# A decoder-layer kernel on one core: the pooling products moved right behind the sums of u in two heads, and the conditioning bursts spread 6, 7, 7

## The chip, the cores and the metric

The kernel runs on one core of a Trainium2 chip. The time is device microseconds of one execution. The kernel before was timed three times: 1939.01, 1940.36 and 1944.08 us, median 1940.36 us. A further execution was recorded by the hardware profiler; every row of the profile comes from that one.

The engines of the core work side by side and each keeps its own order: PE (matrix products; PEld is its weight load), DVE (elementwise work on vectors), ACT (activations, copies and casts), POOL (some elementwise work; it also issues many of the DMAs), SP (issues the other DMAs). An engine never overtakes its own order: if one instruction waits, everything behind it on that engine waits too. Engines wait for each other through semaphores.

## The reference, cut to what matters

One decoder layer on 320 token columns (256 of a prompt, 64 of eight samples), in float32:

```
mod = silu(c) @ w_ada + b_ada                      # conditioning, six vectors of 2048 for each sequence
h   = rmsnorm(x) * (1 + sc1) + sh1
q, k, v, og, u, ga, gb = split(h @ w_in)           # four heads; 11 blocks of 256 columns for each head
y_a = rmsnorm(gated_linear_attention(q, k, v)) * silu(og)     # chunked, with a state for each sequence
d   = trailing_mean(u, window 2, 4, 8 or 16 by head) - u
y_b = (d @ w_pool) * pool_scale                    # the pooling products
x   = x + g1 * ((sigmoid(ga) * y_a + sigmoid(gb) * y_b) @ w_o)
x   = x + g2 * ffn(rmsnorm(x) * (1 + sc2) + sh2)
```

The attention states, the last pooling rows and the normalised output are returned as well.

## The kernel before, in words

Every weight is split into two parts, `whi` (cast by ACT, L162) and `wlo` (what is left, subtracted by DVE, L163), and every product is three matmuls (`mm3`, L177 to L179) of 128 columns of weights against 320 tokens. One projection (`proj`) makes 256 output columns from 16 blocks of input: 96 matmuls, which fill one accumulator `ps`. The accumulators of the projections come from a pool, `pmain`, that holds two; a projection can start when an accumulator has been emptied. Smaller products use another pool, `pmisc`, with four.

The mixer is the stretch between the head of the program and the product with `w_o`. It goes through the four heads. For each head a loop runs over 11 units (one projection each): in heads 1 and 2 the order is gb, gb, q, k, v, v, u, og, og, ga, ga; head 3 has gb last. Head 0 is projected in the head of the program, so its attention and pooling run beside the projections of head 1, those of head 1 beside the later units of head 1 and the first of head 2, and so on.

What runs beside is a list of closures, `queue`. `pump(RATE)` writes up to ten of them after each unit. The attention of a head is `gla_steps` (28 steps). Those that the text below names:

- `s_attP`, `s_kpn`, `s_inter`, `s_oback`: the samples' attention: a masked product (L831; mask on DVE and ACT, L835 to L838), the product with the loaded state (L854, L857; the state tiles `S0` are loaded by POOL's DMAs, L847, 1 MB each), its copy on ACT (L864), four transposes (L133) and copies on DVE (L870).
- `s_state`: new states. Four products into four tiles of `pmisc` (L884, each cleared first by a DVE memset, L879), then four DVE updates (L889) that empty them; the result goes out by a POOL DMA (L890).
- `s_att`, `s_nat`: the prompt's attention scores (DVE L745, PE L756 and L762) and transposes of v (L133).

The pooling of a head is `pool_steps`. It gives four steps `pst`: load the carried rows (L450), transpose them into u (`s_hist`, L460), transpose the last rows of u for output (`s_buf`: POOL copies L468 and L469, transposes L133, DVE copy L474, nine small POOL DMAs L476 and L477), and the window sums (`s_win`, DVE L486 to L500, then the split of d into `dh` on ACT, L353, and `dl` on DVE, L354). And it gives one step `psy`, the pooling products (`s_y`): it takes both accumulators of `pmain`, here named `psy`, makes four sets of six matmuls with `w_pool`, and empties each set by one DVE instruction (L516), which also multiplies by the gate gb. In head 0 `sig0` computes the gates first.

`ada_burst` (L317) is 16 matmuls that make a piece of `mod`. Its 2 MB of weights, `araw`, lie in one buffer during the mixer; two POOL DMAs (L285) refill it once the burst before has read it. `BURST_UNITS` says behind which units of heads 1 to 3 a burst stands, `LOAD_UNITS` where the loads are written.

The program order that all this writes is not yet the engines' order. A scheduler sets that: it goes by the program order, lets an instruction pass others when those cannot start in its own estimate of time, and hands out pool buffers in program order. A matmul that needs a `pmain` accumulator therefore comes behind the matmuls of the two accumulators that were handed out earlier.

Of the kernel before, what the change touches and what calls it, by code (L numbers as in the profile page):

```python
# [34 lines left out]
PSY = 12  # L35
# [42 lines left out]
def body(tc, A):  # L78
# [106 lines left out]
    def proj(w, col, k0, k1, xh, xl, between=None, raw=None):  # L185

        ps = pmain.tile([P, 2, 512], F32, tag="pm", name=nm("ps"))
        for c0 in range(k0, k1, 4):
            nk = min(4, k1 - c0)
            parts = [(i, c0 + j, whi, wlo) for j, whi, wlo in split_chunk(rows(w, col, c0, nk), nk, 256, raw)  # L190
                     for i in range(2)]
            for i, kt, whi, wlo in parts:
                mm3(ps[:, i, :T], whi[:, i * P:(i + 1) * P], wlo[:, i * P:(i + 1) * P],
                    xh[kt], xl[kt], kt == k0, kt == k1 - 1)
            if between:
                between(c0 - k0)
        return ps
# [91 lines left out]
    def anchor(src):  # L289

        return G.tensor_copy(tick, src).ins

    def ada_load(n, bufs, tag="big"):

        if n < len(BURSTS) and n not in ada_raw:
            sec, b, nb, k0, nk = BURSTS[n]
            t = ada_raw[n] = apool[0].tile([P, nk, nb * P], F32, tag=tag, bufs=bufs, name=nm("araw"))
            ada_want.extend((n, t, r) for r in range(0, nk, min(nk, 16 // nb)))

    def ada_all(after=None):  # L300
        while ada_want:
            ada_piece(after)

    def ada_burst():

        n = len(ada_done)
        sec, b, nb, k0, nk = BURSTS[n]
        ada_done.append(n)
        w = nb * P
        if k0 == 0:  # L310
            ada_ps[:] = [misc()]
        ps = ada_ps[0]
        first = True
        with tc.high_priority(), tc.issue_after(last_mm[0]):
            for r in range(nk - 4, -1, -4):
                for j in range(4):
                    PE.matmul(ps[32 * j:32 * j + 32, 0:w], lhsT=scT[:, k0 + r + j, :], rhs=ada_raw[n][:, r + j, :],  # L317
                              start=k0 == 0 and first, stop=k0 + nk == KT and r == 0, tile_position=(0, 32 * j))
                first = False
        if k0 + nk < KT:  # L320
            return
        pt = misc()
        for q in range(0, nb, 2):
            wq = min(2, nb) * P
            sb = apool[0].tile([P, wq], F32, tag="adasb", name=nm("adasb"))
            S.copy(sb, ps[:, q * P:q * P + wq])
            for i in range(wq // P):
                tr(pt[:, (q + i) * P:(q + i + 1) * P], sb[:, i * P:(i + 1) * P])
        blk = sec * KT + b
        V.tensor_reduce(mod[:, blk:blk + nb, :], pt[:, 0:w].rearrange("p (b j r) -> p b r j", b=nb, j=4)[:, :, 0:9, :],  # L330
                        axis=AX.X, op=ALU.add)
        if b == KT - nb:
            dst = mod[:, sec * KT:(sec + 1) * KT, :]
            bb = bada[:, sec * KT:(sec + 1) * KT].unsqueeze(2).broadcast_to([P, KT, 9])
            V.tensor_tensor(dst, dst, bb, op=ALU.add)
            if sec == 4:
                V.tensor_scalar(dst, dst, 1.0, None, op0=ALU.add)
                V.tensor_tensor(dst, dst, N2G.unsqueeze(2).broadcast_to([P, KT, 9]), op=ALU.mult)
# [30 lines left out]
    def new_group(h):  # L369
        g = G0()  # L370
        g.h = h
        g.q = gp.tile([P, 2, T], F32, tag="q", name=nm("q"))
        g.k = gp.tile([P, 2, T], F32, tag="k", name=nm("k"))
        g.v = gp.tile([P, 4, T], F32, tag="v", name=nm("v"))
        g.u = gp.tile([P, 2, UEW], F32, tag="u", name=nm("u"))
        g.gb = merged[h]
        return g

    def new_gates(g):
        g.og = gp.tile([P, 4, T], F32, tag="og", name=nm("og"))  # L380
        g.ga = merged[2] if g.h == 0 else None
# [4 lines left out]
    def evac(ps, g, kind, i, acc):  # L386
        with tc.high_priority():
            evac_now(ps, g, kind, i, acc)
# [29 lines left out]
    def gates(g, kind, i, src):  # L418
        if kind == "gb":
            S.activation(g.gb[:, 2 * i:2 * i + 2, :], src, AF.Sigmoid)  # L420
            return
        og = g.og[:, 2 * i:2 * i + 2, :]
        sg = gp.tile([P, 2, T], F32, tag="sg", name=nm("sg"))
        S.activation(sg, src, AF.Sigmoid)
        if kind == "og":
            V.tensor_tensor(og, src, sg, op=ALU.mult)
        else:
            G.tensor_tensor(og, og, sg, op=ALU.mult)

    def units(h):  # L430
        return [("q", 0, OQ + DK * h), ("k", 0, OK_ + DK * h), ("v", 0, OV + DV * h),
                ("v", 1, OV + DV * h + 256), ("u", 0, OU + 256 * h),
                ("og", 0, OOG + DV * h), ("og", 1, OOG + DV * h + 256),
                ("ga", 0, OGA + DV * h), ("ga", 1, OGA + DV * h + 256),
                ("gb", 0, OGB + DV * h), ("gb", 1, OGB + DV * h + 256)]
# [85 lines left out]
    with tc.tile_pool(name="head", bufs=1) as xp:  # L521
# [55 lines left out]
        g0 = new_group(0)  # L577
# [17 lines left out]
        for si, (k0, k1) in enumerate(SLICES):  # L595
# [11 lines left out]
            for ui, pair in enumerate(us):  # L607
# [9 lines left out]
                if last and ui == 0:  # L617
                    pst, psy = pool_steps(g0)
# [301 lines left out]
    def merge_step(g, E):  # L920
        def f():
            for e in range(4):
                o = E["o"][:, e]
                V.tensor_tensor(o, o, g.og[:, e], op=ALU.mult)
                V.tensor_tensor(g.gb[:, e], o, g.gb[:, e], op=ALU.add)
        return f

    queue = []

    def pump(n):  # L930
        for _ in range(min(n, len(queue))):
            queue.pop(0)()
# [3 lines left out]

    st, E = gla_steps(g0)
    def sig0():
        for kind in ("og", "ga", "gb"):
            for i in range(2):  # L940
                gates(g0, kind, i, getattr(g0, kind)[:, 2 * i:2 * i + 2, :])
    queue += pst + st[:PSY] + [sig0] + st[PSY:] + psy + [merge_step(g0, E)]
    RATE = 10
    BURST_UNITS = (None, (1, 3, 9, 10), (0, 2, 3, 4, 5, 7, 9, 10), (1, 2, 3, 4, 6, 7, 9, 10))
    LOAD_UNITS = (None, (0, 1, 7, 9, 10)) + BURST_UNITS[2:]
    for h in range(1, H):
        pump(RATE)
        g = new_group(h)
        st, E = gla_steps(g)
        order = units(h) if h == 3 else units(h)[9:] + units(h)[:9]  # L950
        for ui, (kind, i, col) in enumerate(order):
            if kind == "og" and i == 0:
                pump(len(queue))
                new_gates(g)
            ps = proj(win, col, 0, KT, hh, hl)
            evac(ps, g, kind, i, None)
            if kind == "v" and i == 1:
                pump(len(queue))
                queue += st
            if kind == "u":  # L960
                pst, psy = pool_steps(g)
                queue[:0] = pst
            if ui in BURST_UNITS[h]:
                ada_burst()
            if ui in LOAD_UNITS[h] and len(ada_done) < AMIX:
                ada_load(len(ada_done), 1)
                done = g.og if kind == "ga" else getattr(g, kind)
                ada_all(None if ui in BURST_UNITS[h] else anchor(done[:, 2 * i, PB:PB + 1]))
            pump(RATE)
            if kind == "v" and i == 0:  # L970
                pump(len(queue))
                queue += [st.pop(0) for _ in range(4)]
                pump(len(queue))
        queue += psy + [merge_step(g, E)]
    pump(len(queue))


# [196 lines left out]
```

## Time and profile before

| | |
|---|---|
| median of three runs | 1940.36 us |
| profiled execution | 1944.37 us, span from first to last instruction 1942.6 us |
| mean granted TensorE clock | 0.995 |
| PE busy | 1895.9 us (98%) |
| DVE, ACT, POOL busy | 1016.3 us (52%), 807.1 us (42%), 146.4 us (8%) |

In the rows, `out<-in` are tiles under the program's names without buffer numbers, `xN` is a count, and `[t <-X]` is how long the engine sat idle before the row and what ended that. The chain of waits is the work that ended last, followed back from the end: its rows say what each stretch of time was spent on. In the list of waits a row reads: engine, tile and line that waited, what released it, then total us, times, longest.

### The profile page before, as it was taken

How to read it: one execution, taken by the hardware profiler on the slowest of the kernel's cores; microseconds unless marked ns; L12 is line 12 of the kernel's file. 1: busy time of each engine (PE TensorE's matmuls, PEld its weight loads, DVE VectorE, ACT ScalarE, POOL GpSimd, SP SyncE). 2: the span in 40 equal slices, each digit the busy share in tenths (PEclk: the TensorE clock that was granted, in tenths of full speed). 3: DMA queues.
4: the chain of work that ended last, by engine and by line, in shares of the span. 5: the costliest groups of instructions: out<-in, count | busy, mean ns of one | idle time of the engine just before them, and what ended most of it. 6: DMA issues, size and time to landing. Idle time of an engine off the chain costs nothing.

```text
span 1942.6 us, 34331 instructions
## 1 busy us (share of the span) xinstructions
PE 1895.9 (98%) x13696; PEld 1795.6 (92%) x13696; DVE 1016.3 (52%) x1974; ACT 807.1 (42%) x1442; POOL 146.4 (8%) x288
## 2 busy tenths in 40 slices
PE   5999999999999999999999999999999999999997
PEld 3888898988998899889989999999999999999997
DVE  4775564656355646555574444444444444444454
ACT  3333363544354444454453343343333434344443
POOL 1110121021011102101020000000000000000000
PEclk9999999999999999999999999999999999999998
DMA  9996556677766777588644555444545444445553
GB/s 345 357 351 231 199 211 230 206 254 255 256 248 216 248 251 272 191 287 311 222 163 152 185 185 186 143 149 147 152 147 155 149 152 152 148 147 151 147 153 103
DMA packets 107328, 398.54 MB, mean 205 GB/s; under 512 B 12084, under 2 KB 20720, under 8 KB 94872
## 3 DMA queue, kind: packets, MB, share of 16 engines
q1 hardware_dynamic: 82480, 261.73, 42.1%
q0 software_dynamic: 24400, 134.54, 18.2%
q8 instruction: 107, 1.75, 0.4%
q14 instruction: 53, 0.43, 0.1%
q10 hardware_dynamic: 288, 0.08, 0.0%
HBM read 374.48 MB, written 22.05 MB: 204 GB/s over the span
## 4 chain that ended last, share of the span: by engine, by line
PE 87%; DMA 2%; DVE 1%; issue 0%; POOL 0%; ACT 0%; DVEq 0%; POOLq 0%; ACTq 0%
PE ps L177 26%; PE ps L178 26%; PE ps L179 26%; PE pm L317 3%; DMA araw<-w_ada 2%; PE pm L133 1%; PE pm L857 1%; PE pm L819 1%; PE pm L808 0%; PE pm L178 0%; PE pm L179 0%; PE pm L177 0%; PE pm L884 0%; DVE yg L1125 0%; PE pm L662 0%
## 5 line engine op out<-in xcount | busy, mean ns | idle before, releaser
L163 DVE TENSOR_TENSOR wlo<-raw,whi 128x512 fp32r<-128x512 f32 x953 | 661.2, 697 | 764.4 <-ACT whi L162 745.7
L162 ACT CAST whi<-raw 128x512 fp32r<-128x512 f32 x953 | 589.7, 621 | 956.5 <-PE ps L178 873.6
L177 PE MATMUL ps<-hh,whi 128*128 128x320 f32 x1408 | 443.3, 315 | 4.2 <-ACT hh L353 2.9
L179 PE MATMUL ps<-hh,wlo 128*128 128x320 f32 x1408 | 439.9, 313 | 2.3 <-DVE wlo L163 2.3
L178 PE MATMUL ps<-hl,whi 128*128 128x320 f32 x1408 | 440.6, 313 | 0.0
L178 PE MATMUL ps<-h2l,whi 128*128 128x320 f32 x1408 | 435.2, 309 | 0.0
L177 PE MATMUL ps<-h2h,whi 128*128 128x320 f32 x1408 | 435.1, 309 | 0.0
L179 PE MATMUL ps<-h2h,wlo 128*128 128x320 f32 x1408 | 434.7, 309 | 0.0
L177 PEld LDWEIGHTS ps<-hh,whi 128*128 128x128 f32 x1408 | 266.3, 189 | 17.9 <-issue 9.5
L178 PEld LDWEIGHTS ps<-hl,whi 128*128 128x128 f32 x1408 | 266.5, 189 | 9.3 <-issue 8.8
L179 PEld LDWEIGHTS ps<-hh,wlo 128*128 128x128 f32 x1408 | 266.3, 189 | 7.9 <-issue 4.8
L177 PEld LDWEIGHTS ps<-h2h,whi 128*128 128x128 f32 x1408 | 264.6, 188 | 3.4 <-ACT ah L353 3.4
L178 PEld LDWEIGHTS ps<-h2l,whi 128*128 128x128 f32 x1408 | 264.8, 188 | 0.1
L179 PEld LDWEIGHTS ps<-h2h,wlo 128*128 128x128 f32 x1408 | 264.7, 188 | 0.0
L179 PE MATMUL ps<-ah,wlo 128*128 128x320 f32 x660 | 203.2, 308 | 0.0
L178 PE MATMUL ps<-al,whi 128*128 128x320 f32 x660 | 203.2, 308 | 0.0
L177 PE MATMUL ps<-ah,whi 128*128 128x320 f32 x660 | 203.1, 308 | 0.0
L178 PEld LDWEIGHTS ps<-al,whi 128*128 128x128 f32 x660 | 123.8, 188 | 0.0
L177 PEld LDWEIGHTS ps<-ah,whi 128*128 128x128 f32 x660 | 123.7, 187 | 0.0
L179 PEld LDWEIGHTS ps<-ah,wlo 128*128 128x128 f32 x660 | 123.7, 187 | 0.0
L177 PE MATMUL ps<-mh,whi 128*128 128x320 f32 x256 | 79.3, 310 | 0.2 <-DVE mg L516 0.2
L178 PE MATMUL ps<-ml,whi 128*128 128x320 f32 x256 | 79.3, 310 | 0.0
(274 smaller groups left out, 1516.6 us busy)
## 6 DMA issues: line engine op xcount, KB each, us to landing
raw<-w_gu SPq DMA_DIRECT2D x176, 512.0 KB, 3.9
raw<-w_in SPq DMA_DIRECT2D x154, 512.0 KB, 4.6
araw<-w_ada POOLq DMA_DIRECT2D x64, 1024.0 KB, 8.9
raw<-w_down SPq DMA_DIRECT2D x79, 512.0 KB, 3.6
hraw<-w_ada POOLq DMA_DIRECT2D x28, 1024.0 KB, 8.4
S<-state_gla POOLq DMA_DIRECT2D x16, 1024.0 KB, 7.8
o_gs<-S POOLq DMA_DIRECT2D x16, 1024.0 KB, 8.4
raw<-w_o SPq DMA_DIRECT2D x32, 512.0 KB, 5.9
```

The lines of the kernel that those rows point to most:

```text
L133: PE.transpose(out, in_, ident[:k, :k])
L162: S.copy(hi, raw)
L163: V.tensor_sub(lo, raw, hi.bitcast(F32))
L177: PE.matmul(ps, lhsT=whi, rhs=xhi, start=start, stop=False)
L178: PE.matmul(ps, lhsT=whi, rhs=xlo, start=False, stop=False)
L179: last_mm[:] = [PE.matmul(ps, lhsT=wlo, rhs=xhi, start=False, stop=stop).ins]
L317: PE.matmul(ps[32 * j:32 * j + 32, 0:w], lhsT=scT[:, k0 + r + j, :], rhs=ada_raw[n][:, r + j, :], start=k0 == 0 and first, stop=k0 + nk == ...
L819: PE.matmul(pt, lhsT=E["kdn"][:, s, d * P:(d + 1) * P], rhs=E["vn"][:, s], start=s == 0, stop=s == 1)
L857: PE.matmul(pt[32 * j:32 * j + 32, :], lhsT=qeP[:, d, 4 * gg + j, :], rhs=E["S0", gg, d][:, j], start=False, stop=d == 0, tile_position=(0 ...
```

## The change

Four edits in the mixer's order. The instructions stay the same; only their places change.

```diff
     def sig0():
-        for kind in ("og", "ga", "gb"):
+        for kind in ("gb", "og", "ga"):
...
-    queue += pst + st[:PSY] + [sig0] + st[PSY:] + psy + [merge_step(g0, E)]
+    queue += pst + st[:PSY] + [sig0] + psy + st[PSY:] + [merge_step(g0, E)]
     RATE = 10
-    BURST_UNITS = (None, (1, 3, 9, 10), (0, 2, 3, 4, 5, 7, 9, 10), (1, 2, 3, 4, 6, 7, 9, 10))
-    LOAD_UNITS = (None, (0, 1, 7, 9, 10)) + BURST_UNITS[2:]
+    BURST_UNITS = (None, (1, 3, 5, 7, 9, 10), (0, 2, 4, 5, 7, 9, 10), (1, 2, 4, 6, 7, 9, 10))
+    LOAD_UNITS = (None, (0, 1, 3, 5, 7, 9, 10)) + BURST_UNITS[2:]
...
             if kind == "u":
                 pst, psy = pool_steps(g)
-                queue[:0] = pst
+                queue[:0] = pst + (psy if h < 3 else [])
...
-        queue += psy + [merge_step(g, E)]
+        queue += (psy if h == 3 else []) + [merge_step(g, E)]
```

In head 0 the pooling products come behind the gates and ahead of the rest of the attention. In heads 1 and 2 they come directly behind the window sums, that is, behind the unit u and ahead of the unit og; head 3 keeps them at the end. The 20 bursts of heads 1 to 3 are spread 6, 7, 7 instead of 4, 8, 8.

What this does to the engines' order shows at three places. First PE in head 1, around the end of unit u. Before, the last product of u (`ps_4049`) is followed by products of og (`ps_4413`), and the samples' attention stands between them:

```order
L179 MATMUL ps_4413<-hh_85,wlo_4417 128x320
L177 MATMUL ps_4413<-hh_86,whi_4416 128x320
L139 MATMUL pm_4024<-identr,kdP 128x128 x2
L178 MATMUL ps_4413<-hl_102,whi_4416 128x320
...
L854 MATMUL pm_4028<-vp_3989,attR 128x512
L857 MATMUL pm_4028<-S_637_3946,qeP 32x512 x4
L857 MATMUL pm_4028<-S_636_3944,qeP 32x512 x4
L178 MATMUL ps_4413<-hl_107,whi_4454 128x320
```

Now, with u named `ps_4078` and og `ps_4482`:

```order
L179 MATMUL ps_4078<-hh_100,wlo_4188 128x320
L133 MATMUL pm_3963<-cst,adasb_3964 128x128 x2
...
L139 MATMUL pm_4053<-identr,kdP 128x128 x2
L854 MATMUL pm_4057<-vp_4018,attR 128x512
...
L133 MATMUL pm_4232<-cst,w_681_4226 128x128 x2
L884 MATMUL pm_4306<-vp_4018,w_653_4052 128x512
...
L177 MATMUL psy_4263<-dh_4259,whi_4267 128x320
...
L179 MATMUL psy_4264<-dh_4259,wlo_4272 128x320
L762 MATMUL pm_4360<-w_645_3996,EX_3773 128x128 x2
L133 MATMUL pm_4367<-cst,v_2703 128x128 x4
L133 MATMUL pm_4373<-cst,v_2703 128x128 x4
L177 MATMUL ps_4482<-hh_85,whi_4485 128x320
```

No product of a projection stands between the last of u and the first of og any more: all the samples' attention of the first four sequences, eight products L884, the 24 pooling products, L756, L762 and the transposes of v follow each other directly. In head 2 the same holds from the transposes L133 behind L857 on; the steps up to L857 still stand among the products of u.

Second, DVE in head 1 at the same place. Now the window sums (`w_684`, `w_685`, `w_686`), which the pooling products wait for, stand among the state updates L889, here from the second set of four on:

```order
L889 SCALAR_TENSOR_TENSOR S_642_3975<-S_642_3975,dec_3772,pm_4323 128x512
L889 SCALAR_TENSOR_TENSOR S_642_3975<-S_642_3975,dec_3772,pm_4322 128x512
L889 SCALAR_TENSOR_TENSOR S_642_3975<-S_642_3975,dec_3772,pm_4321 128x512
L486 TENSOR_TENSOR w_685_4249<-w_684_4246 128x2x453
L889 SCALAR_TENSOR_TENSOR S_642_3975<-S_642_3975,dec_3772,pm_4320 128x512
L495 SCALAR_TENSOR_TENSOR w_686_4251<-w_685_4249,u_2704 128x2x256
L497 SCALAR_TENSOR_TENSOR w_686_4251<-w_685_4249,u_2704 128x64 x2
L499 TENSOR_TENSOR w_686_4251<-w_685_4249,cst 128x16 x2
L500 TENSOR_TENSOR w_686_4251<-w_686_4251,u_2704 128x16 x2
L745 TENSOR_TENSOR w_705_4338<-EQK_3771,EX_3773 128x384 x2
L354 TENSOR_TENSOR dl_4260<-w_686_4251,dh_4259 128x640
```

Before, the same instructions stood there in the same sequence, with splits of weights (L163) and an evacuation of og among them:

```order
L889 SCALAR_TENSOR_TENSOR S_637_3946<-S_637_3946,dec_3769,pm_4252 128x512
L486 TENSOR_TENSOR w_680_4220<-w_679_4217 128x2x453
L889 SCALAR_TENSOR_TENSOR S_637_3946<-S_637_3946,dec_3769,pm_4251 128x512
L163 TENSOR_TENSOR wlo_4701<-raw_4698,whi_4700 128x512
L495 SCALAR_TENSOR_TENSOR w_681_4222<-w_680_4220,u_2704 128x2x256
L497 SCALAR_TENSOR_TENSOR w_681_4222<-w_680_4220,u_2704 128x64 x2
L163 TENSOR_TENSOR wlo_4705<-raw_4698,whi_4704 128x512
```

So the chain on DVE from the state updates to `dl` did not move in itself; the products that wait for it did.

Third, PE in head 0's pooling products. Before, they stood behind unit q of head 1 (`ps_3245`), with L884 among them:

```order
L179 MATMUL ps_3245<-hh_100,wlo_3355 128x320
L177 MATMUL psy_3401<-dh_2594,whi_3405 128x320
L178 MATMUL psy_3401<-dl_2595,whi_3405 128x320
L179 MATMUL psy_3401<-dh_2594,wlo_3406 128x320
L177 MATMUL psy_3401<-dh_2594,whi_3409 128x320
L884 MATMUL pm_2924<-vp_2847,w_456_2881 128x512
```

Now they stand two units earlier, behind the first gb unit (`ps_2705`), and L688 of the attention stands ahead of the next unit (`ps_2995`):

```order
L179 MATMUL ps_2705<-hh_100,wlo_2815 128x320
L177 MATMUL psy_2900<-dh_2594,whi_2904 128x320
...
L179 MATMUL psy_2901<-dh_2594,wlo_2909 128x320
L688 MATMUL pm_2621<-cumr,w_409_2607 128x272
...
L688 MATMUL pm_2639<-cumr,w_409_2607 128x400
L177 MATMUL ps_2995<-hh_85,whi_2998 128x320
```

The first 18 of the 24 products go there; the other six stand 21 products of `ps_2995` later. In head 3, where the pooling products keep their place, the mixer's last burst moves in among them: 56 matmuls of 128x320 stand between the last two bursts instead of 66.

## The prediction

> **What bounds the kernel now.** I read the page first, then PE's waits, then PE in order of time around the pooling products.
>
> ```profile
> span 1942.6 us, 34331 instructions
> ...
> PE 1895.9 (98%) x13696; PEld 1795.6 (92%) x13696; DVE 1016.3 (52%) x1974; ACT 807.1 (42%) x1442; POOL 146.4 (8%) x288
> ```
>
> ```profile
> PE pm L317 <- DMA araw<-w_ada: 3.0, 4, 1.8
> ...
> PE psy L177 <- ACT sg L424: 1.5, 1, 1.5
> ...
> PE ps L177 <- DVE mg L516: 1.2, 2, 0.9
> ...
> PE psy L177 <- DVE mg L516: 1.0, 1, 1.0
> ```
>
> PE is the bound; 46.7 us of the span are not busy, most of it in the head. The waits above, and one of 2.0 us below, are all that the change can remove: at the pooling products (`psy`, and `ps` behind them) 1.5, 1.2 and 1.0 us, at the bursts 3.0 us. The longest has a tail, in PE's order of time:
>
> ```profile
> 293.71 0.64 PE L177 MATMUL psy<-dh,whi 128*128 128x320 f32 x1 [2.00 <-DVE pm L879]
> 294.14 0.47 PE L178 MATMUL psy<-dl,whi 128*128 128x320 f32 x1
> 294.41 0.47 PE L179 MATMUL psy<-dh,wlo 128*128 128x320 f32 x1
> ...
> 297.70 0.31 PE L177 MATMUL ps<-hh,whi 128*128 128x320 f32 x1
> 297.85 0.31 PE L178 MATMUL ps<-hl,whi 128*128 128x320 f32 x1
> ```
>
> Start to start a matmul takes 0.15 us (297.70 to 297.85), but 0.27 us for some 3 us behind a wait of 2.0 us. This wait so cost about 3.9 us. The Trainium skill ("TensorE: Matmul & The Clock Gate", section "Why this matters for your kernels") has the drop to half clock only behind idle gaps above about 3 us; the row shows it behind 2.0, and the row decides. By that rule the sum below would be 1.4 us lower, since the waits of about 2 us would leave no slow stretch.
>
> **Gains.** Head 0: the products move behind the first gb unit. The wait of 3.9 us goes. Two smaller ones come: the second half of `psy_2900` waits for L516 on the first half (the 0.31 us that the last product takes, less its 0.15, plus 0.55; about 0.8 with the hand-overs, I take 0.9), and `psy_2901` needs the accumulator of the gb unit, which ACT empties late:
>
> ```profile
> 250.14 1.29 PE pm L662 x6
> ```
>
> ```profile
> 257.25 0.71 ACT L420 ACTIVATE mg<-ps 128x640 f32<-128x640 f32 x1
> ```
>
> ```profile
> 295.71 0.55 DVE L516 SCALAR_TENSOR_TENSOR mg<-psy,vec,mg 128x320 f32<-128x320 f32 x1 [1.53 <-PE psy L179]
> ```
>
> L662 ends at 251.4, and 21 products of the gb unit follow it: PE is through at 254.4. Six pooling products, the wait, six more: 256.9. ACT has emptied the gb unit at 257.96 (before, and nothing ahead of it on ACT has moved), so PE waits 1.1. Gain 3.9 - 2.0 = 1.9 us. Heads 1 and 2: the waits at the old places go, 1.0 and 1.5 + 0.9 = 3.4 us. Burst waits that the wider spread removes: two small ones of the four, 0.6 us. Together 5.9 us.
>
> **Cost in head 1.** Both accumulators belong to `psy` until it is emptied, so PE has no projection to run between u and og. What it does meanwhile hangs on a chain through DVE and ACT which products of og hid before. Its durations:
>
> ```profile
> 371.82 0.64 PE pm L139 x8
> ...
> 376.94 0.90 PE pm L831 x8
> ...
> 382.66 1.85 PE pm L857 x16
> ...
> 388.23 0.86 PE pm L133 x8
> 394.67 0.43 PE pm L884 x3
> ...
> 417.20 1.01 PE pm L756 x32
> 418.21 0.64 PE pm L762 x4
> ```
>
> ```profile
> 379.35 0.35 DVE L838 SCALAR_TENSOR_TENSOR attR<-attR,vec,attP 128x128 fp32r<-128x128 f32 x1
> ...
> 388.70 0.48 DVE L870 COPY EQK<-pm 128x32 f32<-128x32 f32 x4 [0.80 <-PE pm L133]
> 389.11 0.46 DVE L460 COPY u<-pm 128x120 f32<-128x120 f32 x2
> 389.49 0.41 DVE L474 COPY nb<-pm 128x256 f32<-128x256 f32 x1
> ...
> 390.54 1.08 DVE L486 TENSOR_TENSOR w<-u 128x908 f32<-128x908 f32 x1
> ...
> 395.14 0.75 DVE L889 SCALAR_TENSOR_TENSOR S<-S,dec,pm 128x512 f32<-128x512 f32 x1 [1.14 <-PE pm L884]
> ...
> 403.35 2.06 DVE L889 SCALAR_TENSOR_TENSOR S<-S,dec,pm 128x512 f32<-128x512 f32 x3
> 405.32 1.10 DVE L486 TENSOR_TENSOR w<-w 128x906 f32<-128x906 f32 x1
> 406.34 0.74 DVE L889 SCALAR_TENSOR_TENSOR S<-S,dec,pm 128x512 f32<-128x512 f32 x1
> ...
> 407.60 0.69 DVE L495 SCALAR_TENSOR_TENSOR w<-w,u 128x512 f32<-128x512 f32 x1
> 408.20 0.36 DVE L497 SCALAR_TENSOR_TENSOR w<-w,u 128x64 f32<-128x64 f32 x2
> ...
> 413.66 0.82 DVE L354 TENSOR_TENSOR dl<-w,dh 128x640 fp32r<-128x640 f32 x1
> 414.52 1.03 DVE L745 TENSOR_TENSOR w<-EQK,EX 128x384 f32<-128x384 f32 x2
> ```
>
> ```profile
> 384.58 0.59 ACT L864 COPY osn<-pm 128x512 f32<-128x512 f32 x1 [1.46 <-PE pm L857]
> ```
>
> ```profile
> L353 ACT CAST dh<-w x4: 717/723/727, 248.2 to 782.6; 128x640 fp32r<-128x640 f32 x4
> ```
>
> Time from u's last product, by the engines' new order. PE does its transposes and L831 until 2.6 (two, eight and four transposes at 0.11 to 0.08, 0.90, two more). The mask is ready 1.9 later (L831 ends at 377.84, the last L838 at 379.70): 4.6. L854 and L857, 0.2 + 1.85: 6.7. L864: 7.4. Eight transposes: 8.3. DVE follows them with L870, L460, L474 (the tail of the last two) and L486: 10.5. Only then, after the memsets on DVE, come four L884; L889 starts 0.47 later (394.67 to 395.14) and takes 2.8 for four: 13.9. `pmisc` is full until then, so the second four L884 wait for it: 14.0. Three L889, L486, L889: 14.5 + 2.1 + 1.1 + 0.7 = 18.3. L495, L497, and the pairs L499 and L500 on 16 columns (less than L497's 0.36 each; I take 0.25): 19.6. `dh` on ACT: 20.3. `dl` on DVE behind L745, 1.0 + 0.8: 21.3. Twelve pooling products, ten of them at the slow 0.27: 24.0. L756, slow: 25.5. The other twelve at 0.15, behind L516: 27.3. L762 and the transposes of v, 0.4 + 0.9: 28.6. Then og starts.
>
> PE's own work in these 28.6 us at full clock is 0.2 + 0.64 + 0.44 + 0.90 + 0.2 + 2.1 + 0.86 + 0.86 + 3.5 + 1.0 + 0.6 + 0.9 = 12.2. Lost: 16.4 us, plus 0.7 for L884 at half clock behind waits of 2 and 3 us. 17.1 us.
>
> **Cost in head 2.** L857 still stands among products of u, so the count starts at L864. The transposes of u's last rows wait for ACT's evacuation of u and four POOL copies behind the issue of L450: 2.5. Behind DVE's L474 and L486 L884 starts at 4.5; from there it goes as above with one more window sum (1.1): two sets of L889, three L486, `dl` at 16.6, og at 23.9. PE's work inside: 7.6. Lost 16.3 + 0.7 = 17.0 us.
>
> These two terms carry the forecast. They rest on order and duration, not on a guess about contention. Bounds for each: at least 10 us, if DVE runs a fifth faster when it splits no weights, and the first steps overlap u's end; at most 21, if the slow clock lasts two stretches of 3.4 us longer.
>
> **Small costs.** In head 3 the last burst now comes behind 56 matmuls instead of 66. Its weights land late already, in the chain of waits:
>
> ```profile
> 854.83 1.91 PE pm L317 x32
> ...
> 857.54 10.70 DMA araw<-w_ada
> ```
>
> The burst ahead ends at 856.74, the weights land at 868.24, 11.5 us later. Ten matmuls are 1.5 us, so PE waits that much longer: 1.5 us (between 0 and 4: the load may find an idle queue, or the clock may drop behind the wait). The other bursts cost PE the same wherever they stand. Their loads, two DMAs on POOL's queue each, are issued when the burst ahead has read the buffer; at one unit's distance (96 products, 14 us) 11.5 us are covered, and in heads 1 and 2 POOL issues none of them between a state's store and the load that follows it. The load of `w_pool` on SP's queue moves ahead of og's weights by one place; og starts 24 us and more behind u, so its weights have landed, and the two splits of `w_pool` on ACT and DVE take the place of two of og's. `sig0`'s order changes ACT's work by nothing: the same six sigmoids in one row. On DVE, L163 for og queues behind the window sums; only og waits for it, and that waits for the accumulator longer. Past the mixer nothing moves.
>
> **Sum.** 17.1 + 17.0 + 1.5 - 5.9 = 29.7 us. The profiled execution would go from 1944.4 to 1974; it stands 4.0 us above the median of the runs, which so goes from 1940.4 to 1970.
>
> **Rivals.** (a) Faster: the pooling chain hides under PE's own pieces, and only gains remain, 1940.4 - 5.9 + 1.5 = 1936. DVE, 52% busy, has room. Decides: the stretch from u to og must shrink from 28.6 to 12.2 us and from 23.9 to 7.6. Against it: 9 us of L889 and window sums alone stand in sequence on DVE. (b) Slower still: L857 of the second four sequences waits for its state. POOL loads it only when the store of the state before is done:
>
> ```profile
> 407.38 0.77 POOL L890 DMA_DIRECT2D o_gs<-S  x1 [2.80 <-DVE S L889]
> ...
> 421.59 0.75 POOL L847 DMA_DIRECT2D S<-state_gla  x1 [9.87 <-DMA o_gs<-S]
> ```
>
> 14 us for the store, about 9 for the load: in head 1 ready at 18.3 + 14 + 9 = 41, wanted at about 37; head 2 36 against 32. With 4 us in each and colder clocks 1978 to 1988. Against it: the queues carry less while PE stands. (c) DVE's stretch shrinks below the lower bounds: 1946 to 1955. (d) The scheduler's order is kept but the waits overlap so far that gains and losses cancel: within 6 us of 1940.
>
> Chances: the forecast, 1955 to 1985, 0.80; (b) above 1985, 0.08; (c) 0.06; (a) 0.03; (d) 0.03. 0.3%, about 6 us, is what a measurement of this kernel can tell. Slower so has 0.94. The range is the forecast's own, which leaves 0.20 out: 10 us in each head give 1956, 21 give 1978, and the upper end takes in most of (b).
>
> **What would show it.** In heads 1 and 2 PE waits between u and og for DVE's L879, L889 and L354 or ACT's `dh`, 14 to 20 us in each, with slow matmuls behind; the granted clock falls below 0.995; PE's busy time changes little, the span by 30 us. At 254 us two waits of about 1 us. No wait at `psy` behind ga. The forecast is wrong if og's products start within 15 us of u's end, or if PE waits longest for a DMA.

## The result

The changed kernel took 1968.95 us (median of 4 runs, 1968.08 to 1969.99); the kernel before took 1941.88 us in the runs beside it. The ratio is 1.0134, with a 95% interval of 1.0119 to 1.0149: 27.1 us slower, where 29.7 had been forecast. The profiled execution has a span of 1967.5 us and a mean granted clock of 0.988 (0.995 before).

From the page and the list of waits of the changed kernel (what waited, what released it, total us, times, longest):

```profile
PE 1897.4 (96%) x13696; PEld 1797.4 (91%) x13696; DVE 1018.1 (52%) x1974; ACT 807.3 (41%) x1442; POOL 146.6 (7%) x287
```

```profile
PE psy L177 <- ACT dh L353: 12.9, 2, 7.0
PE pm L884 <- DVE pm L879: 9.7, 4, 2.9
...
PE pm L857 <- DMA S<-state_gla: 2.9, 1, 2.9
...
PE pm L854 <- DVE attR L838: 1.5, 1, 1.5
...
PE pm L133 <- POOL w L468: 1.4, 1, 1.4
...
PE psy L177 <- ACT mg L420: 1.1, 2, 0.8
...
PE psy L177 <- DVE mg L516: 0.6, 1, 0.6
PE pm L317 <- DMA araw<-w_ada: 0.4, 1, 0.4
```

PE's busy time is nearly the same (1897.4 against 1895.9 us); the added time is waiting. PE stands idle for 70.1 us of its span in place of 46.7, 23.4 us more. Five kinds of these waits stand in the two places that the forecast named: `dh`, L879, L838, L468 and a wait of 0.7 us for L864 make 26.2 us. PE in head 1, from u's last product to og's first, in the order of time:

```profile
377.79 0.31 PE L179 MATMUL ps<-hh,wlo 128*128 128x320 f32 x1
...
382.02 0.47 PE L854 MATMUL pm<-vp,attR 128*128 128x512 f32 x1 [1.53 <-DVE attR L838]
...
385.05 0.66 PE L133 MATMUL pm<-cst,osn 128*128 128x128 f32 x4 [0.70 <-ACT osn L864]
...
388.31 0.51 PE L884 MATMUL pm<-vp,w 32*128 32x512 f32 x4 [2.17 <-DVE pm L879]
391.71 0.80 PE L884 MATMUL pm<-vp,w 32*128 32x512 f32 x4 [2.90 <-DVE pm L879]
398.34 0.90 PE L177 MATMUL psy<-dh,whi 128*128 128x320 f32 x2 [5.83 <-ACT dh L353]
...
406.97 0.39 PE L177 MATMUL ps<-hh,whi 128*128 128x320 f32 x1
```

u ends at 378.10 and og starts at 406.97, 28.9 us later. Between them PE waits five times, 13.1 us in all, for a step on DVE or ACT that itself stood behind a step on PE: the engines take turns. The same in head 2:

```profile
596.00 0.31 PE L179 MATMUL ps<-hh,wlo 128*128 128x320 f32 x1
...
598.35 0.50 PE L133 MATMUL pm<-cst,w 128*128 128x128 f32 x2 [1.40 <-POOL w L468]
600.61 0.51 PE L884 MATMUL pm<-vp,w 32*128 32x512 f32 x4 [1.75 <-DVE pm L879]
604.01 0.80 PE L884 MATMUL pm<-vp,w 32*128 32x512 f32 x4 [2.90 <-DVE pm L879]
611.85 0.90 PE L177 MATMUL psy<-dh,whi 128*128 128x320 f32 x2 [7.04 <-ACT dh L353]
...
619.63 0.39 PE L177 MATMUL ps<-hh,whi 128*128 128x320 f32 x1
```

596.31 to 619.63 is 23.3 us, with 13.1 us of waiting. What DVE and ACT do meanwhile in head 1, the second set of updates and the window sums, is one row of work without an idle gap behind 392.54:

```profile
392.54 2.06 DVE L889 SCALAR_TENSOR_TENSOR S<-S,dec,pm 128x512 f32<-128x512 f32 x3 [0.89 <-PE pm L884]
394.52 1.10 DVE L486 TENSOR_TENSOR w<-w 128x906 f32<-128x906 f32 x1
395.54 0.74 DVE L889 SCALAR_TENSOR_TENSOR S<-S,dec,pm 128x512 f32<-128x512 f32 x1
```

```profile
397.57 0.72 ACT L353 CAST dh<-w 128x640 fp32r<-128x640 f32 x1 [12.57 <-DVE w L500]
```

One wait is new and was not in the forecast, in head 0: L857 waits 2.9 us for a loaded state. POOL's queue before (first fence) and after (second), each from the first store of a state to the load that L857 waits for:

```profile
293.49 0.77 POOL L890 DMA_DIRECT2D o_gs<-S  x1 [22.78 <-DVE S L889]
298.18 0.77 POOL L847 DMA_DIRECT2D S<-state_gla  x1 [3.93 <-DMA o_gs<-S]
301.17 0.76 POOL L890 DMA_DIRECT2D o_gs<-S  x1 [2.22 <-DVE S L889]
307.06 1.09 POOL L285 DMA_DIRECT2D araw<-w_ada  x2 [5.13 <-PE pm L317]
308.13 0.76 POOL L847 DMA_DIRECT2D S<-state_gla  x1
```

```profile
292.72 0.77 POOL L890 DMA_DIRECT2D o_gs<-S  x1 [25.45 <-DVE pm L879]
301.56 0.77 POOL L847 DMA_DIRECT2D S<-state_gla  x1 [8.07 <-DMA o_gs<-S]
302.32 0.76 POOL L890 DMA_DIRECT2D o_gs<-S  x1
303.07 1.08 POOL L285 DMA_DIRECT2D araw<-w_ada  x2
315.11 0.76 POOL L847 DMA_DIRECT2D S<-state_gla  x1 [10.96 <-DMA o_gs<-S]
```

```profile
324.31 2.97 PE L857 MATMUL pm<-S,qeP 128*32 128x512 f32 x16 [2.90 <-DMA S<-state_gla]
```

The first store took 4.7 us before and 8.8 now. While the load waits for it, the second store and the burst's weights queue up behind the load on POOL and then go out together; the second store takes 12.8 us (302.32 to 315.11, when the load that waits for it goes out), and the last load is issued 7 us later than before. L857 itself then takes 2.97 us where the forecast's row had 1.85, at a granted clock of 0.63, and the products right behind it run at 0.50.

### The profile page after: what moved, and what is told of

Same layout as the page of the kernel before. It is cut to its first block, busy times and chain, and to the rows that moved or that the text cites. A ratio compares the mean times of both kernels' runs of the same rounds, so it can differ in the third digit from the quotient of the medians.

```text
span 1967.5 us, 34326 instructions
## 1 busy us (share of the span) xinstructions
PE 1897.4 (96%) x13696; PEld 1797.4 (91%) x13696; DVE 1018.1 (52%) x1974; ACT 807.3 (41%) x1442; POOL 146.6 (7%) x287
## 4 chain that ended last, share of the span: by engine, by line
PE 81%; DMA 3%; issue 2%; DVE 1%; ACT 0%; POOL 0%; DVEq 0%; POOLq 0%
PE ps L177 24%; PE ps L178 24%; PE ps L179 24%; PE pm L317 3%; DMA araw<-w_ada 1%; DMA S<-state_gla 1%; PE pm L133 1%; PE pm L857 1%; DMA o_gs<-S 1%; PE pm L819 1%; DVE S L889 0%; PE pm L884 0%; PE psy L177 0%; PE pm L179 0%; PE pm L177 0%
## 5 line engine op out<-in xcount | busy, mean ns | idle before, releaser
L163 DVE TENSOR_TENSOR wlo<-raw,whi 128x512 fp32r<-128x512 f32 x953 | 658.7, 694 | 765.2 <-ACT whi L162 754.8
```

The source lines that it names most:

```text
L163: V.tensor_sub(lo, raw, hi.bitcast(F32))
```

## The experiments

All ratios are to the kernel before, run beside the kernel in question, with a 95% interval. The kernel before had medians from 1939.75 to 1944.71 us in these comparisons, so ratios are to be compared, not times. Two theories stood against each other at first. The first is the forecast's: in heads 1 and 2 PE has no projection to run, and waits for a chain through DVE and ACT. The rival: the other edits disturb loads and queues, and the waits at u only show it.

**The products of heads 1 and 2 put back.** The changed kernel without its third edit:

```diff
-                queue[:0] = pst + (psy if h < 3 else [])
+                queue[:0] = pst
...
-        queue += (psy if h == 3 else []) + [merge_step(g, E)]
+        queue += psy + [merge_step(g, E)]
```

> The changed kernel with the pooling products of heads 1 and 2 put back to their old place; head 0's move and the new burst tables stay. Theory (PE has nothing to run between u and og, and waits for DVE's and ACT's chain): the profile of the changed kernel has 28.9 us from u's end to og's start in head 1 and 23.5 in head 2, with 12.2 and 7.6 us of PE work in them, so 32.6 us go; the old waits at psy, 3.4 us, come back. 1969 - 32.6 + 3.4 = 1940, between 1937 and 1943. Rival (the loss comes from loads and queues disturbed by the other edits, and the stall at u only shows it): the time stays above 1955.

Measured: 1941.78 us, ratio 1.0002 (0.9992 to 1.0012). The whole loss goes with this edit, and the rival falls. From 1.0134 to 1.0002 is 25.6 us, less than the 29 expected. Part of the rest is in its trace: the bursts wait 4.4 us again, where the changed kernel's wait 0.4.

```profile
PE pm L317 <- DMA araw<-w_ada: 4.4, 3, 1.9
```

The two longest of them, 1.74 and 1.92 us, stand in head 3 (at 835.77 and 861.94), more than 200 us behind the place of head 2's stall. So the stalls did not simply cover these loads; why bursts wait less in the changed kernel stays open.

**The burst tables alone.** The kernel before with the two changed tables.

> The kernel before with the new burst tables alone. The changed kernel has a wait of 2.9 us for a state load in head 0 (L857 for S), with a slow stretch behind it, about 4.7 us, that the prediction had not; and its waits at bursts fell from 3.0 to 0.4 us. Theory A (the burst at an earlier unit issues its load right behind the state's store, which then takes longer, so the next state load starts late): this kernel has the wait too, -2.5 + 4.7 gives about 1944. Theory B (head 0's earlier pooling products are the cause): no such wait here, -2.5 gives 1939. The prediction's own terms for the bursts (-0.6 + 1.5) give 1943 without that wait.

Measured: 1939.37 us, 0.9995 (0.9985 to 1.0005): nothing that can be told from no change. Its L857 waits 0.2 us, so theory A falls. The burst waits go from 3.0 to 2.2 us.

**More work on DVE, in both kernels.** In heads 1 and 2 four more sums that write the same values again, on line 491, right behind the last window sum:

```diff
-                cur = t
+                prev, cur = cur, t
...
-            w = WINDOWS[h]
+            w = WINDOWS[h]; [V.tensor_tensor(t[:, :, w // 2:], prev[:, :, w // 2:], prev[:, :, 0:UEW - w // 2], op=ALU.add) for _ in range(4 if h in (1, 2) else 0)]
```

> The changed kernel with four more window sums on DVE in heads 1 and 2, which write the same values once more, right behind the last sum. Theory (DVE's chain to dl and ACT's dh is what PE waits for): four sums of about 1.02 us start to start in each head, 2 x 4.1 = 8.2 us more, 1977, between 1975 and 1980; the wait of psy for dh grows by 4 us in each head. Rival (the end of the stall is set by something else, the weights of w_pool or a DMA): within 2 us of 1969.

Measured in the changed kernel: 1977.49 us, 1.0182 (1.0167 to 1.0198), 8.5 us above 1968.95 by the medians, 9.3 by the ratios. The sums and the wait in head 1:

```profile
394.59 4.51 DVE L491 TENSOR_TENSOR w<-w 128x906 f32<-128x906 f32 x4
```

```profile
401.30 0.90 PE L177 MATMUL psy<-dh,whi 128*128 128x320 f32 x2 [10.38 <-ACT dh L353]
```

4.51 us of DVE lengthen the wait from 5.83 to 10.38, by 4.55; in head 2 from 7.04 to 11.57. Within the spread of the runs, every microsecond that DVE works longer there is a microsecond of the kernel.

> The kernel before with the same four more window sums on DVE in heads 1 and 2 that cost the changed kernel 8.5 us. Theory (there the products of og and the units behind it cover DVE's chain): within 2 us of before, 1938 to 1942. Rival (DVE's work costs time wherever it stands): 1948.

Measured in the kernel before: 1935.87 us, 0.9968 (0.9953 to 0.9984). The sums cost nothing, and the kernel is faster by 5 to 6 us. The sums cannot be the reason; what changed with them is the order. The scheduler, presumably because it counts DVE as busy for longer, splits the pooling products of heads 1 and 2 into pieces of 6, 12 and 6, with four L884 between the first two and L903 and a burst between the last two. The waits at `psy` and `ps` behind L424 and L516 in heads 1 and 2, 3.4 us, are not in its trace any more, and bursts wait less:

```profile
PE pm L317 <- DMA araw<-w_ada: 1.2, 2, 0.7
```

**The products later by one, two and three units.** The changed kernel with the products of heads 1 and 2 written behind the first og unit, the second, and the first ga unit:

```diff
-            if kind == "u":
-                pst, psy = pool_steps(g)
-                queue[:0] = pst + (psy if h < 3 else [])
+            if kind == "u": pst, psy = pool_steps(g); queue[:0] = pst
+            if (kind, i) == ("og", 0) and h < 3:     # then ("og", 1), then ("ga", 0)
+                queue[:0] = psy
```

> The changed kernel with the pooling products of heads 1 and 2 one unit later, behind the first og unit. Theory (the loss is PE work missing beside a chain of fixed length): one unit is 96 products of 0.147 us, 14.1 us, of cover in each head, so 16.7 us become about 2.6 and 15.9 about 1.8: 1969 - 28 = 1941, between 1938 and 1946. Rival (both accumulators waiting for dh cost the same wherever they stand, or the chain grows longer beside the splits of og's weights): above 1955.

Measured: 1961.74 us, 1.0097 (1.0080 to 1.0114). The expectation missed by 21 us. One unit gave back some 7 us, not 28; the time is where the rival put it, above 1955.

```profile
396.49 0.50 PE L884 MATMUL pm<-vp,w 32*128 32x512 f32 x4
401.29 0.80 PE L884 MATMUL pm<-vp,w 32*128 32x512 f32 x4 [4.29 <-DVE pm L879]
407.92 0.90 PE L177 MATMUL psy<-dh,whi 128*128 128x320 f32 x2 [5.83 <-ACT dh L353]
```

The unit does run in between, but the chain is no longer of fixed length. Its own steps on PE (L831, L857, L133, the first L884) now stand in line among og's products, and DVE splits og's weights among its steps. From u's end (376.91) to the first pooling product it takes 31.0 us, against 20.2 in the changed kernel (the next expectation has 29.6 for this stretch, which the trace does not bear out); in head 2, 24.4 against 15.5. Of 14.1 us of cover 10.8 and 8.9 went into a longer chain. The end of the chain, from the second L884 to `dh`, is as bare as before: PE waits 5.83 us for `dh` in head 1 again, and 8.4 us in head 2 (7.0 in the changed kernel).

> The changed kernel with the pooling products of heads 1 and 2 two units later, behind the second og unit. One unit gave back 7 us only, not 28: in it the chain's own PE links (L831, L857, L133, L884) stand in line among og's products, so the chain to dh took 29.6 us from u's end in head 1 in place of 20.2. Theory (what counts is which projection products stand behind the chain's last PE link, the second four L884, and ahead of the pooling products: none there, 39 here in head 1 and 85 in head 2, 5.7 and 12.5 us, against the 6.6 to 8.9 us from that link to dh): about 1 us of waiting in head 1, none in head 2, and 1938 to 1943. Rival (each unit gives back 3 to 4 us in each head): about 1954.

Measured: 1946.12 us, 1.0029 (1.0013 to 1.0044), between the two theories' numbers. In head 2 the wait is gone, in head 1 it is 3.1 us, not 1, and the bursts wait 5.6 us, which the expectation did not have:

```profile
PE pm L317 <- DMA araw<-w_ada: 5.6, 3, 3.1
PE psy L177 <- ACT dh L353: 3.1, 1, 3.1
```

The rule it was to test holds in kind: what counts is the projection work behind the chain's last PE step and ahead of the products that need its result.

> The changed kernel with the pooling products of heads 1 and 2 three units later, behind the first ga unit. No wait for dh in either head, and gb's gates and both halves are ready: the old waits at psy (1.7 and 1.1 us in head 2, 1.0 in head 1) go too. 1936 to 1941 with the state wait of head 0 in it. Rival (a new wait at psy for L516 of 1 us a head, or the pooling products push head 1's second half of the attention later): 1942 to 1946.

Measured: 1941.46 us, 1.0003 (0.9989 to 1.0016). The time lies between the two ranges. There is no wait for `dh`, but head 2 has a new one, of 2.7 us. It is of another kind than the rival's, which was for L516:

```profile
PE ps L177 <- DVE pm L879: 2.7, 1, 2.7
```

**Head 0's move alone.**

> The kernel before with head 0's move alone (gb's gates first, pooling products behind the first gb unit). The prediction's term: 3.9 us go, two waits of 0.65 and 0.80 us come in all runs with this move so far, so -1.9 to -2.5 and 1937.5 beside a before of 1939.8. The wait of L857 for the second state load of head 0 (2.9 us in the changed kernel, 1.4 with head 0's move and the new bursts, 0.2 with the new bursts alone): theory A, the move itself shifts the first state's store to where weight loads run, so this kernel has the wait too, 1 to 3 us and its slow stretch, and stands within 2 us of before; theory B, it needs the burst's load at the same place as well, then no such wait and 1937 to 1938.

Measured: 1941.98 us, 1.0011 (0.9995 to 1.0027). The old wait of 2.0 us with its slow stretch is gone, the two small ones are there, and L857 waits 1.4 us for its state: theory A. A third small wait comes with the move, 0.77 us of a product for its split weight (L163). The move saves at the old place what was forecast and loses it again at the state load and this wait.

To see whether the state load's wait is worth the difference, the stores that the load waits for were made smaller: for the first group of head 0 this kernel writes the first of four sequences and leaves out the other three:

```diff
-                nc.gpsimd.dma_start(A["o_gs"][0, 4 * gg:4 * gg + 4, ...
+                n = 1 if h == 0 and gg == 0 else 4; nc.gpsimd.dma_start(A["o_gs"][0, 4 * gg:4 * gg + n, ...
```

> Head 0's move alone, but in head 0 the stores of the first four sequences' states write one sequence of four each (0.25 MB in place of 1 MB, the rest of that output is left out). Head 0's move alone stood at 1942.0 beside a before of 1941.2, with a wait of 1.4 us at L857 for the state load and about 1.6 us of slow products behind it, because the load on POOL's queue waits 8.0 and 10.2 us for the stores (3.9 and none in the kernel before). Theory (the move's gain of about 2 us was eaten by this wait): no wait at L857, some 3 us less than head 0's move, 1938.5 to 1939.5 beside a before of 1941. Rival (the wait is not worth anything: what follows it would wait elsewhere): 1941 to 1942.

Measured: 1940.04 us, 0.9988 (0.9979 to 0.9997). POOL's queue:

```profile
292.43 0.55 POOL L890 DMA_DIRECT2D o_gs<-S  x1 [25.42 <-DVE pm L879]
296.27 0.77 POOL L847 DMA_DIRECT2D S<-state_gla  x1 [3.29 <-DMA o_gs<-S]
299.53 0.55 POOL L890 DMA_DIRECT2D o_gs<-S  x1 [2.50 <-DVE S L889]
301.35 1.06 POOL L285 DMA_DIRECT2D araw<-w_ada  x2 [1.27 <-PE pm L317]
305.55 0.76 POOL L847 DMA_DIRECT2D S<-state_gla  x1 [3.15 <-DMA o_gs<-S]
```

The last load goes out at 305.55 instead of 313.64 (head 0's move alone), L857 no longer waits, and the kernel is 2.3 us faster than before, near the 1.9 of the forecast. (No run has the small stores without the move, so a part of the 2.3 us may come from the small stores alone.) Why the store became slow is settled in part. By the view of the DMA queues, SP's queue, which loads w_in at that time, moved 1.05 MB in the 8.8 us of the store's own 1.05 MB, in head 0's move alone and in the changed kernel alike. In the 4.7 us that the store took in the kernel before, it moved 0.06 MB. The Trainium skill ("DMA: Bandwidth & Descriptors", section "Issuing engines are not separate DMA queues") says that transfers issued by different engines run on the same 16 DMA engines and interleave; the two store times, 4.7 and 8.8 us for the same megabyte, agree with that. No run took the loads of w_in away, so that they are the cause is likely, not shown.

**One accumulator at a time.** The forecast said that PE has no projection because both accumulators belong to `psy`. Here the products are two steps with one accumulator each; in heads 1 and 2 the second goes behind the first og unit. (Lines behind 507 stand two or three later, so L886 is L884 and L881 is L879.)

```diff
-            pp = [pmain.tile([P, 2, 512], F32, tag="pm", name=nm("psy")) for _ in range(2)]
-            for ee in range(4):
+            pp = {half: pmain.tile([P, 2, 512], F32, tag="pm", name=nm("psy"))}
+            for ee in (2 * half, 2 * half + 1):
...
-                queue[:0] = pst + (psy if h < 3 else [])
+                queue[:0] = pst + (psy[:1] if h < 3 else [])
+            if (kind, i) == ("og", 0) and h < 3: queue[:0] = psy[1:]
```

> The changed kernel with the pooling products of every head in two steps that take one accumulator each; in heads 1 and 2 the first step stays behind u and the second goes behind the first og unit, so one accumulator is free for og while the first half waits for dh. In the built order og's products still stand behind the first pooling product: 20 of them come between it and the next ones. Theory of the prediction taken alone (og is kept away because both accumulators belong to the pooling products): a good part of the 14.1 us of og's first unit runs ahead, 1941 to 1955. Rival (with an accumulator free, the order still has the first pooling product, which waits for dh, ahead of og, so what is lost is fixed by that place): the waits for L879 and dh stay, only the later, slow pooling products find other work around them, 1962 to 1969, psy waiting some 6 and 7 us for dh again.

Measured: 1964.63 us, 1.0109 (1.0087 to 1.0132). The waits for `dh` and L879 are those of the changed kernel to the tenth, 12.9 and 9.7 us:

```profile
387.16 0.80 PE L886 MATMUL pm<-vp,w 32*128 32x512 f32 x4 [2.90 <-DVE pm L881]
393.78 0.64 PE L177 MATMUL psy<-dh,whi 128*128 128x320 f32 x1 [5.83 <-ACT dh L353]
394.22 0.47 PE L177 MATMUL ps<-hh,whi 128*128 128x320 f32 x1
```

og's first product runs at 394.22 directly behind the first pooling product, so its accumulator and its first weights were there; the order had it behind. Two accumulators in use are not what is needed to keep og away. The place in PE's order is enough. This kernel stood some 4 to 5 us below the changed one, and its trace has that in head 0: L859 (L857 in the others) waits 0.2 us for its state in place of 2.9, with no slow stretch behind it, and the wait of 0.77 us for a split weight is gone.

**Towards a better kernel.** The first attempt writes the pooling products of the kernel before under the scheduler's high priority, to have them in pieces without useless work on DVE:

```diff
-                    mm3(ps, whi[:, ee * P:(ee + 1) * P], wlo[:, ee * P:(ee + 1) * P],
+                    with tc.high_priority(): mm3(ps, whi[:, ee * P:(ee + 1) * P], wlo[:, ee * P:(ee + 1) * P],
```

> The kernel before with the pooling products written under the scheduler's high priority, so that half of them move in among the products of the last unit, and 24 products of the next unit stand ahead of the last six; nothing else changes place by the program. The waits of heads 1 and 2 at psy (1.0 in head 1; 1.5 and 0.9 in head 2) should shrink to about 1 us in all; head 0's 2.0 us stay, since its products stay beside L884. 1938 to 1940 beside a before of 1941; rival (the waits only move, or the state loads come later): 1941 to 1942.

Measured: 1945.38 us, 1.0015 (1.0006 to 1.0024), a little slower and above both ranges. The waits for L516 are gone, but L424 is waited for in two heads (3.0 us) and the bursts wait 5.6 us.

The second adds the new tables to the four sums in the kernel before:

> The kernel before with four more window sums on DVE in heads 1 and 2 stood at 0.9968 of before (0.9953 to 0.9984), not because of the sums: the scheduler, which sees DVE later, puts the pooling products in four parts between L884, L903 and a burst, and the waits at psy in heads 1 and 2 and all but 1.2 us of those at bursts are gone from its trace. This kernel adds the new burst tables, under which head 2 and 3 have a burst less. Theory (the order of the pooling products is what pays, the tables nothing): 1935 to 1937, 0.996 to 0.998. Rival (the tables' gain of 0.8 us in burst waits adds up with it): 1934 to 1935. If the gain was chance, 1939 to 1941.

Measured: 1940.82 us, 0.9995 (0.9986 to 1.0004). Neither theory, but the time of the third case, in which the gain was chance: with other bursts the scheduler's order in head 1 is another one, and a wait of 2.7 us for L879 appears there, beside 3.8 us at bursts. The kernel before with the four sums stays the fastest kernel that was run, 0.3% ahead of before and 1.6% ahead of the changed kernel. Its gain goes with one built order: the waits that are gone from its trace make 5.2 us, of the 5 to 6 that it gains. No run here reached that order without the sums.

## Why the prediction was right, point by point

| step | forecast, us | measured, us |
|---|---|---|
| head 1, u's end to og's start | 28.6, less 12.2 of PE's work, plus 0.7 slow clock: 17.1 lost | 28.9, less 12.2: 16.7 |
| head 2, the same | 23.9, less 7.6, plus 0.7: 17.0 lost | 23.3, less 7.6: 15.7 |
| head 0's products | -1.9 | -3.9 + 0.65 + 0.80 = -2.4 |
| old waits at psy in heads 1 and 2 | -3.4 | -3.4, none left |
| bursts | -0.6 + 1.5 = +0.9 | 3.0 to 0.4: -2.6 |
| state load of head 0 | not in the sum | 2.9 + 1.5 slow = +4.4 |
| sum | 29.7 | 28.4 |

From L662 in head 1's first unit (at 249.98 and 247.16) to the end the two traces take 1692.6 and 1720.4 us, 27.8 us apart; the medians differ by 27.1. 0.8 us more than the table has is the wait in head 0 for a split weight, which comes with the move. That makes 29.2, and some 1.4 us the other way stay unassigned. They do not lie in a wait: the waits that came and went add up to the 23.4 us by which PE's idle time grew.

**The two large terms** came from PE's built order and from durations of the profile before, and the losses hold to 0.4 and 1.3 us. The steps hold one by one: L854 was forecast 4.6 us behind u's end and its wait ended at 3.9, the first four L884 at 10.5 and came at 10.2, the second at 14.0 and came at 13.6. `dh` was forecast at 20.3 and the first product that needs it came at 20.2; `dl` at 21.3, and its first product came at 21.2 (399.26). One sign missed: PE was to wait 14 to 20 us in each head and waited 13.1, and slow products took more of the loss than forecast. That the chain is what PE waits for is shown by the four added sums, which cost 8.5 us here and nothing before; that the edit in heads 1 and 2 carries the loss, by taking it back (1.0002).

**Both accumulators.** The attribution was too narrow: with one accumulator free the waits were the same. The reading that held was the plainer one, that no projection product stands between u and og in PE's order.

**Head 0** held as a term (2.4 us at the old place and the two new waits) and failed in the sum: it brought the split weight's 0.8 us and the state load's 4.4 us, which the sum does not have. For the load, the step "in heads 1 and 2 POOL issues none of them between a state's store and the load that follows it" looked at heads 1 and 2 only. In head 0 the products' move put a slow store, the load that waits for it and a burst's weights in one row on POOL.

**The bursts** were forecast with the wrong sign. The mixer's last burst, in head 3, waited 0.56 us before and was to wait 1.5 us longer. In the changed kernel it does not wait at all: it starts at 888.69, 9.1 us behind the end of the burst ahead, where the forecast had 11.5 us until its weights land. (The 0.36 us in the list belong to the burst ahead of it.) With the products of heads 1 and 2 put back the same burst waits 1.92 us, close to the forecast. The tables alone change nothing (0.9995), and burst waits range from 0.4 to 5.6 us over these kernels, so such a term cannot be read from the distance in matmuls alone; what else sets it, no run shows. Two errors, +4.4 for the state load and -3.5 for the bursts, nearly cancelled: that the sum came within 3 us is partly luck, the two large terms are not.

**Rivals.** (b), state loads late in heads 1 and 2, did not come. The forecast took 14 us for a store there; in head 1, with PE standing, POOL's loads followed the stores by 6.4 and 4.9 us (391.83 to 398.21 and 396.57 to 401.48), and L857 waited in neither head. The same mechanism struck in head 0, where PE was not standing. (a), (c) and (d) fell with the measured stretches.

## What to carry to other kernels

When a consumer is moved next to its producer, look in the busy engine's built order at what stands between them. If nothing independent does, the whole chain through the other engines is paid, and durations from the old profile gave the price to 0.4 and 1.3 us of 17 here. Independent work helps in full only behind the chain's last step on the busy engine; of 14.1 us put in ahead of that, 3 to 5 us came back, because it lengthened the chain. And a queue that alternates a store with a load that waits for it has to be read at every place that the change shifts, not only where instructions move.

## What the runs showed of the hardware

The half clock behind a wait of 2 us is not certain. The kernel before with the four sums (first fence) and the one with the new tables (second) have the same wait of 1.99 us at the same instruction; behind it the first steps 0.27 us from product to product at a granted clock of 0.51, and the second 0.15 at 1.00:

```profile
290.98 0.60 PE L177 MATMUL psy<-dh,whi 128*128 128x320 f32 x1 [1.99 <-DVE pm L879]
291.37 0.47 PE L178 MATMUL psy<-dl,whi 128*128 128x320 f32 x1
```

```profile
290.26 0.42 PE L177 MATMUL psy<-dh,whi 128*128 128x320 f32 x1 [1.99 <-DVE pm L879]
290.52 0.31 PE L178 MATMUL psy<-dl,whi 128*128 128x320 f32 x1
```

The forecast took the slow stretch behind 2.0 us as certain; it is one of two outcomes, worth 1.5 us here: from the wait's end to the next unit's first product it takes 4.00 us in the first and 2.51 us in the second. Of four traces with this wait of 2 us, two have the slow stretch (the kernel before is the other); what decides it, no run shows. The waits for `dh` of 5.8 us and longer were each followed by slow products. The rule of the Trainium skill quoted in the forecast ("TensorE: Matmul & The Clock Gate", section "Why this matters for your kernels": no idle gaps above about 3 us) is thus no bound below which a gap is free.
